# Three of seven block products on 512 columns at once, and one of them a tile later, in a two-layer encoder on one core

## The chip, the core and the metric

The kernel runs on one core of a Trainium2 chip. The metric is device time in microseconds, the median of the timed runs. All its arithmetic is float32; matrix products run in TensorE's fp32r format, and each operand is split into a high part (rounded to fp32r) and a low part (the rest), so that a product is three matmuls: high by high, high by low and low by high.

## The reference, cut to what matters

Two layers of a transformer on 512 tokens of width 1024, each with a gated feed-forward, a mixing block with three kinds of attention, and a second feed-forward. The change lies in the four feed-forwards (two a layer), whose inner width is 2816:

```python
def rms_norm(x, g):
    xf = x.astype(jnp.float32)
    y = xf * lax.rsqrt(jnp.mean(xf * xf, axis=-1, keepdims=True) + EPS)
    return (y * g.astype(jnp.float32)).astype(x.dtype)

def swiglu(h, w_gate, w_up, w_down):
    return (jax.nn.silu(h @ w_gate) * (h @ w_up)) @ w_down
...
        h = rms_norm(x, norm_g[l, 0])
        x = x + 0.5 * swiglu(h, ffn_w_gate[l, 0], ffn_w_up[l, 0], ffn_w_down[l, 0])
```

## The kernel before, in words

Features lie on the 128 partitions and tokens along the free axis: an activation is 8 tiles of 128 x 512. The inner width is cut into 22 tiles of 128 (`MF`), and `ffn` (line 275) goes through them. The first two (in the first feed-forward four) are computed plainly, a gate and an up product of 512 columns each. All others, 18 in the first feed-forward and 20 in each of the three others, 78 in all, go through `seven` (line 418).

`seven` computes a tile's gate and up rows for both halves of the tokens (256 each, `H`) as a two-by-two block product: the gate and up weights, split over the two halves of the 1024 input features, are one matrix of four blocks, the activations another. It does so in seven block products instead of eight, in the manner of Strassen and Winograd. The weights' sums come in by an accumulating DMA (`added`, line 408) and two additions on VectorE (lines 446 and 447); the activations' sums are made once a feed-forward (`Sides`, line 368). Each block product (`block_product`, line 456) has four chunks of 128 features: per chunk a matmul of high weights with the high tokens (line 460) and one with the low tokens (line 461), both 256 columns wide and with the same weights, and then four of the low weights with the high tokens (line 463). That is 12 matmuls of 256 columns a product and 84 a tile.

Three sets of weights are cast a tile (`parted`, line 91): the high part on ScalarE (line 95), the low part on VectorE (line 96). They are called here wa (the gate's weights), w31 (the sums from the DMA) and w24 (the sums made on VectorE, which need wa's buffer). A fourth, half as large, w22, is cast at lines 436 and 437. The results are combined by copies on ScalarE (lines 474, 483, 485), additions on VectorE (487, 490, 491), a multiplication by the tokens' scale (494), Silu on ScalarE (495), the gating (496), and the split of the result into high and low (`keep`, lines 119 and 121), which the down projection reads.

PSUM has eight banks of 2 KB a partition. The tag `mm` has three of them, `s` and `t` two each. A bank holds 512 float32 columns, two block products side by side.

Each engine takes its instructions in the order in which they stand in its queue. That order is set when the program is built, by a scheduler that reorders within what dependencies and the `issue_after` marks allow; a reader of a PSUM bank waits for the last matmul of the product that was put into it. Where an instruction of a queue waits, what stands behind it waits too.

The down projection (lines 336 to 348) reads all 22 tiles, in three chunks of 8, 8 and 6 for each of 8 output tiles; the last feed-forward has its own form of it in `finish` (line 599).

## Time and profile before

| what | value |
|---|---|
| timed runs, median | 2421.22 us (2420.89 to 2421.51, 3 runs) |
| profiled execution, span from its first to its last instruction (the page gives no other time for it) | 2419.2 us |
| TensorE busy | 2404.9 us (99%), 14418 matmuls |
| weight load busy | 2138.0 us (88%) |
| VectorE busy | 1652.9 us (68%) |
| ScalarE busy | 1254.9 us (52%) |
| GpSimd busy | 270.2 us (11%) |
| granted TensorE clock, mean | 0.998 |

In a row of the timeline stand the start in us, the length in us, the engine, the line, the operation, the tiles (out<-in), their shapes and a count. A matmul's recorded length runs beyond the start of the next one, since they are pipelined; what a matmul costs is the distance from its start to the next one's. The same holds for VectorE and ScalarE: the next instruction starts a little before the recorded end of the one ahead, unless it has to wait for it. In brackets stands how long the engine was idle, and what released it.

### The profile page before, as it was taken

The page shows a single profiled execution, that of the slowest core. Times are in us where ns is not written, and L with a number is a line of the kernel's source. Part 1 is how long each engine was busy: PE and PEld are TensorE (multiplying, and loading weights), DVE is VectorE, ACT ScalarE, POOL GpSimd, SP SyncE. Part 2 cuts the span into 40 slices and gives each one's busy share as a digit, 9 for nine tenths or more (in the row PEclk, how much of TensorE's full clock was granted, in tenths as well). Part 3 has the DMA queues.
Part 4 walks back from the last instruction along what each step waited for, and adds up shares of the span by engine and source line. Part 5 has one row for each costly group of instructions (what it writes and reads, how often), then busy time and mean ns, then how long its engine had stood idle before and what let it go on. Part 6 is the DMA issues. An engine that isn't in the chain of part 4 may idle for free.

```text
span 2419.2 us, 37505 instructions
## 1 busy us (share of the span) xinstructions
PE 2404.9 (99%) x14418; PEld 2138.0 (88%) x14418; DVE 1652.9 (68%) x2767; ACT 1254.9 (52%) x2277; POOL 270.2 (11%) x404
## 2 busy tenths in 40 slices
PE   9999999999999999999999999999999999999998
PEld 7999888888888889998899998888888888999987
DVE  7888445766666678884398873467666666888832
ACT  6555225756567445552255552367566674555532
POOL 3100003311000010000010000133110000100000
PEclk9999999999999999999999999999999999999999
DMA  6675444432332457664367754443322324577632
GB/s 198 174 186 162 128 135 124 115 98 80 94 88 80 131 160 183 185 157 143 119 179 183 183 151 131 127 129 104 101 83 87 95 94 131 168 181 182 175 114 70
DMA packets 113298, 327.19 MB, mean 135 GB/s; under 512 B 13464, under 2 KB 18888, under 8 KB 113120
## 3 DMA queue, kind: packets, MB, share of 16 engines
q1 hardware_dynamic: 88896, 247.04, 33.1%
q0 software_dynamic: 23072, 75.90, 14.4%
q8 instruction: 114, 1.87, 0.3%
q10 hardware_dynamic: 1152, 1.86, 0.2%
q14 instruction: 64, 0.52, 0.1%
HBM read 302.69 MB, written 12.62 MB: 130 GB/s over the span
## 4 chain that ended last, share of the span: by engine, by line
PE 98%; ACT 1%; DVE 0%; issue 0%; DMA 0%; SPq 0%; POOLq 0%; POOL 0%; DVEq 0%; ACTq 0%
PE mm L112 9%; PE mm L110 9%; PE mm L109 9%; PE mm L344 5%; PE mm L345 5%; PE mm L347 5%; PE pr L463 5%; PE pr L460 5%; PE mm L460 5%; PE mm L461 5%; PE mm L463 5%; PE pr L461 5%; PE av L847 2%; PE mm L1065 2%; PE mm L1061 2%; PE mm L1060 2%
## 5 line engine op out<-in xcount | busy, mean ns | idle before, releaser
L87 ACT CAST whi<-raw 128x1024 fp32r<-128x1024 f32 (+1 forms) x258 | 265.7, 1031 | 420.9 <-PE mm L345 184.8
L88 DVE TENSOR_TENSOR wlo<-raw,whi 128x1024 fp32r<-128x1024 f32 (+1 forms) x258 | 309.5, 1201 | 229.1 <-ACT whi L87 121.5
L109 PE MATMUL mm<-h,whi 128*128 128x512 f32 x800 | 318.5, 398 | 0.0
L110 PE MATMUL mm<-l,whi 128*128 128x512 f32 x800 | 313.9, 392 | 0.0
L96 DVE TENSOR_TENSOR wlo<-raw,whi 128x1024 fp32r<-128x1024 f32 x156 | 191.1, 1225 | 83.1 <-ACT whi L95 82.9
L345 PE MATMUL mm<-g,whi 128*128 128x512 f32 x528 | 205.4, 389 | 0.0
L344 PE MATMUL mm<-g,whi 128*128 128x512 f32 x528 | 205.4, 389 | 0.0
L112 PE MATMUL mm<-h,wlo 128*128 128x512 f32 x800 | 197.7, 389 | 0.0
L112 PEld LDWEIGHTS mm<-h,wlo 128*128 128x128 f32 x800 | 150.2, 188 | 31.3
L110 PEld LDWEIGHTS mm<-l,whi 128*128 128x128 f32 x800 | 150.5, 188 | 29.1 <-DVE l L141 0.5
L109 PEld LDWEIGHTS mm<-h,whi 128*128 128x128 f32 x800 | 150.4, 188 | 29.0 <-ACT h L139 0.6
L95 ACT CAST whi<-raw 128x1024 fp32r<-128x1024 f32 x156 | 163.9, 1050 | 10.1 <-DMA raw<-in_w_gu 8.0
L460 PE MATMUL pr<-side,whi 128*128 128x256 f32 x624 | 156.5, 283 | 0.0
L461 PE MATMUL pr<-side,whi 128*128 128x256 f32 x624 | 156.5, 283 | 0.0
L461 PE MATMUL mm<-l,whi 128*128 128x256 f32 x624 | 156.5, 283 | 0.0
L460 PE MATMUL mm<-h,whi 128*128 128x256 f32 x624 | 156.4, 283 | 0.0
L415 POOL DMA_DIRECT2D wsum<-in_w_gu x78 | 68.0, 872 | 686.9 <-DVE g L121 255.7
L347 PE MATMUL mm<-g,wlo 128*128 128x512 f32 x528 | 131.4, 389 | 0.0
L474 ACT COPY gu<-mm 128x256 f32<-128x256 f32 x78 | 29.0, 372 | 195.3 <-PE mm L463 195.2
L806 ACT ACTIVATE lg<-lg,negm 128x256 f32<-128x256 f32 (+1 forms) x192 | 114.2, 595 | 26.7 <-DVE negm L803 25.5
L461 PEld LDWEIGHTS mm<-l,whi 128*128 128x128 f32 x624 | 119.8, 192 | 0.2
L460 PEld LDWEIGHTS mm<-h,whi 128*128 128x128 f32 x624 | 119.8, 192 | 0.2
(306 smaller groups left out, 6130.1 us busy)
## 6 DMA issues: line engine op xcount, KB each, us to landing
raw<-in_w_gu SPq DMA_DIRECT2D x94, 512.0 KB, 3.7
wsum<-in_w_gu SPq DMA_DIRECT2D x78, 512.0 KB, 4.1
wsum<-in_w_gu POOLq DMA_DIRECT2D x78, 512.0 KB, 6.6
raw<-in_w_down SPq DMA_DIRECT2D x48, 512.0 KB, 3.6
raw<-in_w_gate SPq DMA_DIRECT2D x48, 512.0 KB, 3.6
raw<-in_w_qk SPq DMA_DIRECT2D x44, 512.0 KB, 3.6
a<-in_w_gu SPq DMA_DIRECT2D x78, 256.0 KB, 4.8
raw<-in_w_branch SPq DMA_DIRECT2D x24, 512.0 KB, 3.5
```

The lines of the kernel that those rows point to most:

```text
L87: nc.scalar.copy(hi[:, w], raw[:, w])
L88: lower[:] = [nc.vector.tensor_tensor(out=lo[:, w], in0=raw[:, w], in1=f(hi[:, w]), op=ALU.subtract).ins]
L96: nc.vector.tensor_tensor(out=lo, in0=src, in1=f(hi), op=ALU.subtract)
L109: nc.tensor.matmul(ps, wh, xhi[k], start=k == 0, stop=False)
L110: nc.tensor.matmul(ps, wh, xlo[k], start=False, stop=False)
L112: nc.tensor.matmul(ps, wl, xhi[k], start=False, stop=k == n - 1)
L344: nc.tensor.matmul(ps, w[k][0], ghi[c + k], start=c + k == 0, stop=False)
L345: nc.tensor.matmul(ps, w[k][0], glo[c + k], start=False, stop=False)
L347: nc.tensor.matmul(ps, w[k][1], ghi[c + k], start=False, stop=c + k == MF - 1)
L460: nc.tensor.matmul(ps, wh[k], bh, start=start and k == 0, stop=False, skip_group_check=True)
L461: nc.tensor.matmul(ps, wh[k], bl, start=False, stop=False, skip_group_check=True)
L463: nc.tensor.matmul(ps, wl[k], bh, start=False, stop=stop and k == 3, skip_group_check=True)
```

## The change

High and low parts of the tokens, which were two tiles, are now two halves of one tile of 128 x 2 x 512 (`both`), and the same holds for the activations' sums (`two`, `both` in `Sides`). A matmul can so read 256 columns of the high part and 256 of the low part in one go, as 512 columns with the same weights: it writes both to one PSUM bank, the high part's result in the left half and the low part's in the right half. The halves are added afterwards, by a copy on ScalarE and an addition on VectorE. Three of the seven products are done like this (`wide`), with 4 matmuls of 512 columns and 4 of 256 instead of 12 of 256. Four products go one after the other through one bank, `one`: the first, the second after that is copied out, a third, and at last the product of w22, which is the wide one and stands in the next tile (`rest`, called by `flush`). With it the gating and the split of a tile's result move into the next tile, and for the last tile into the down projection.

Per tile, 84 matmuls become 72. On VectorE one addition of 256 columns and two of 512 become six of 256; on ScalarE three copies of 256 become five. The sets of weights, their casts and all transfers are as before.

```diff
         def parts(self, k, xk):
             g = self.gain[:, k : k + 1]
-            hi = xpool.tile([P, S], F32R, tag=f"h{k}", name=f"h{k}")
+            both = self.both[k] = xpool.tile([P, 2, S], F32R, tag=f"h{k}", name=f"h{k}")
+            hi, lo = both[:, 0], both[:, 1]
             nc.scalar.activation(hi, xk, AF.Copy, scale=g)
-            lo = xpool.tile([P, S], F32R, tag=f"l{k}", name=f"l{k}")
...
                 for c, n, w in parts:
+                    if m == 0 and c == 8:
+                        tiles.flush()
                     for k in range(n):
...
+            two = fp.tile([P, 2, S], F32R, tag="pair", name="pair", bufs=4)
+            self.halves(one.rearrange("p a c -> p (a c)"), two)
+            both = fp.tile([P, 2, H], F32R, tag="side", name="side", bufs=4)
+            self.halves(t3, both)
+            self.t = [two[:, :, :H], two[:, :, H:], both]
+            self.b11, self.b21, self.b22 = h.both[e][:, :, :H], h.both[o][:, :, :H], h.both[o][:, :, H:]
+            self.t4, self.b12 = t4, h.both[e][:, :, H:]
...
+        def product(self, bank, w, b, start=False, stop=False, wide=True):
...
+            (wh, wl), (ps, both) = w, (bank[:, 0], bank)
...
+            def mm(dst, k, w, b):
+                nc.tensor.matmul(dst, w[k], b, start=start and k == 0 and w is wh and b is not low, stop=False, skip_group_check=True)
...
+            for k, bk in enumerate(b):
+                low = bk[:, 1]
+                if wide:
+                    mm(both, k, wh, bk)
+                else:
+                    mm(ps, k, wh, bk[:, 0])
+                    mm(ps, k, wh, low)
+            for k, bk in enumerate(b):
+                nc.tensor.matmul(ps, wl[k], bk[:, 0], start=False, stop=stop and k == 3, skip_group_check=True)
...
+            self.product(one, blocks(wa), [s.b11 for s in sides], start=True, wide=False)
+            kept = nc.scalar.copy(c11, one[:, 0])
...
+            self.product(two, blocks(w31, S), self.side(1), start=True)
+            nc.scalar.copy(c22, two[:, 1])
+            nc.vector.tensor_tensor(out=c22, in0=two[:, 0], in1=c22, op=ALU.add)
+            done = self.flush()
+            w22 = [fp.tile([P, S], F32R, tag=g, name=g) for g in ("w22h", "w22l")]
+            nc.scalar.copy(w22[0], a22)
+            nc.vector.tensor_tensor(out=w22[1], in0=a22, in1=f(w22[0]), op=ALU.subtract)
+            self.product(one, blocks(w24), self.side(2), wide=False)
+            self.held = [nc.scalar.copy(c12, one[:, 0]).ins]
+            self.product(three, blocks(wa, S), [s.b21 for s in sides], start=True, stop=True, wide=False)
+            nc.vector.tensor_tensor(out=c11, in0=three[:, 0], in1=c11, op=ALU.add)
+            self.product(two, blocks(w24, S), [s.b22 for s in sides], stop=True)
+            for n in range(2):
+                nc.vector.tensor_tensor(out=c12, in0=two[:, n], in1=c12, op=ALU.add)
+            self.product(one, blocks(w31), self.side(3), wide=False)
+            nc.scalar.copy(u3, one[:, 0])
+            gn = g[:, 0:2].rearrange("p a c -> p (a c)")
+            un = g[:, 3:5].rearrange("p a c -> p (a c)")
+            nc.vector.tensor_tensor(out=gn, in0=gn, in1=h.rb, op=ALU.mult)
+            nc.scalar.activation(gn, gn, AF.Silu)
+            nc.vector.tensor_tensor(out=c22, in0=c22, in1=u3, op=ALU.add)
...
+            def rest():
+                self.product(one, blocks(w22), self.side(4), stop=True)
+                nc.scalar.copy(c21, one[:, 1])
+                nc.vector.tensor_tensor(out=c21, in0=one[:, 0], in1=c21, op=ALU.add)
+                last = nc.vector.scalar_tensor_tensor(out=un, in0=un, scalar=-1.0, in1=gn, op0=ALU.mult, op1=ALU.mult)
+                keep(fp, un, *self.out)
+                return last.ins
```

In the changed file the lines are: the matmuls of high weights 437, those of low weights 447; the copies of c11 494, c22 501, c12 508, u3 515 and c21 524; Silu 519; w22's casts 505 and 506; the additions 502, 510, 513 (twice), 520 and 525; the scale 518 and the gating 526; the sums of weights 478 and 479.

The order of ScalarE's queue in a tile in the middle of the second feed-forward, before. A name's number tells the buffers apart: gu_10943 belongs to the tile that is being finished, gu_11069 to the tile that is being computed; whi from raw with the lower number is w24, with the higher number the next tile's wa. In brackets stand the engines and transfers waited for.

```order
L95 CAST whi_11056<-wsum_11041 128x1024 [waits DMAHW0_49,DMASW4_49,Activation_49]
L474 COPY gu_11069<-mm_11066 128x256 [waits DVE_49,PE_49]
L495 ACTIVATE gu_10943<-gu_10943 128x512 [waits DVE_49,Activation_49]
L95 CAST whi_11062<-raw_11044 128x1024 [waits DVE_49]
L119 CAST g_11037<-gu_10943 128x512 [waits DVE_49]
L483 COPY gu_11069<-mm_11066 128x256 [waits PE_49]
L95 CAST whi_11174<-raw_11170 128x1024 [waits DMAHW1_49]
L436 CAST w22h_11178<-a22_11172 128x512 [waits DMAHW2_49,PE_49,Activation_49]
L485 COPY pv_11068<-pr_11067 128x256 [waits PE_49]
```

After, a tile of the same kind (gu_10059 is being finished, gu_10178 computed; whi_10171 is w24, whi_10280 the next tile's wa):

```order
L515 COPY gu_10059<-mm_10056 128x256 [waits PE_49]
L519 ACTIVATE gu_10059<-gu_10059 128x512 [waits DVE_49]
L494 COPY gu_10178<-mm_10175 128x256 [waits PE_49,Activation_49]
L505 CAST w22h_10217<-a22_10159 128x512 [waits DMAHW1_49,PE_49]
L501 COPY gu_10178<-pr_10176 128x256 [waits PE_49]
L524 COPY gu_10059<-mm_10056 128x256 [waits PE_49]
L95 CAST whi_10171<-raw_10157 128x1024 [waits DVE_49]
L119 CAST g_10213<-gu_10059 128x512 [waits DVE_49]
L508 COPY gu_10178<-mm_10175 128x256 [waits PE_49]
L95 CAST whi_10280<-raw_10276 128x1024 [waits DMAHW2_49]
L95 CAST whi_10284<-wsum_10273 128x1024 [waits DMAHW3_49,DMASW0_49,Activation_49]
```

The w24 cast stood behind Silu and now stands behind four instructions that wait for TensorE, the last of them the copy of line 524. 48 tiles have these ahead of it; in 26 it stands as in the next tile, between w22's cast and that copy (whi_10290 is w24 there), and the first tile of each feed-forward has no copy of line 524:

```order
L515 COPY gu_10178<-mm_10175 128x256 [waits PE_49]
L519 ACTIVATE gu_10178<-gu_10178 128x512 [waits DVE_49]
L494 COPY gu_10297<-mm_10294 128x256 [waits PE_49,Activation_49]
L501 COPY gu_10297<-pr_10295 128x256 [waits PE_49]
L505 CAST w22h_10336<-a22_10278 128x512 [waits DMAHW4_49,PE_49]
L95 CAST whi_10290<-raw_10276 128x1024 [waits DVE_49]
L524 COPY gu_10178<-mm_10175 128x256 [waits PE_49]
L508 COPY gu_10297<-mm_10294 128x256 [waits PE_49]
```

In the last of these fences the cast moved one place ahead of the copy. On TensorE, where the product with w24 and side 2 begins, before (the end of w22's product, and the first matmuls that need w24):

```order
L463 MATMUL pv_11068<-h1_8398,w22l_11053 128x256
L463 MATMUL pv_11068<-h2_8441,w22l_11053 128x256
L463 MATMUL pv_11068<-h3_8484,w22l_11053 128x256
L460 MATMUL mm_11066<-side_8677,whi_11062 128x256 [waits Activation_49]
L461 MATMUL mm_11066<-side_8679,whi_11062 128x256
```

And after (the end of the product w22 of the tile before, the one product that follows it, and the first matmul that needs w24):

```order
L447 MATMUL mm_10056<-h3_8335,w22l_10099 128x256
L437 MATMUL pv_10177<-h4_8377,whi_10161 128x256 x2
L437 MATMUL pv_10177<-h5_8419,whi_10161 128x256 x2
L437 MATMUL pv_10177<-h6_8461,whi_10161 128x256 x2
L437 MATMUL pv_10177<-h7_8503,whi_10161 128x256 x2
L447 MATMUL pv_10177<-h4_8377,wlo_10162 128x256
L447 MATMUL pv_10177<-h5_8419,wlo_10162 128x256
L447 MATMUL pv_10177<-h6_8461,wlo_10162 128x256
L447 MATMUL pv_10177<-h7_8503,wlo_10162 128x256
L437 MATMUL mm_10175<-pair_8523,whi_10171 128x256 [waits Activation_49]
```

Between the product whose copy stands ahead of the w24 cast on ScalarE and the product that needs this cast there are now 12 matmuls of 256 columns. In the 26 other tiles one of the twelve stands behind the start of the product with w24.

More of the change, by code (lines that the diff above doesn't have):

```diff
@@ L285, in ffn @@
                 sides = []
-            loads, held = [], ()
+            loads = []
             start, plain = (2, 4) if first else (0, 2)
@@ L293, in ffn @@
                             small_values(fp)
+                    if m == plain:
+                        tiles = Seven(l, i, h, fp, sides, ghi, glo)
                     with tc.issue_after(h.marks[1]):
-                        held, gated_last = seven(l, i, m, h, fp, sides, ghi, glo, loads[1], sums if m == plain else None, held)
+                        gated_last = tiles.tile(m, loads[1], sums if m == plain else None)
                     continue
@@ L383, in __init__ @@
             b11, b12, b21, b22 = t[0][:, :H], t[0][:, H:], t[1][:, :H], t[1][:, H:]
-            one, two = [fp.tile([P, 2, H], F32, tag="g", name="tsum", bufs=GBUFS) for _ in range(2)]
-            t1, t2, t3, t4 = one[:, 0], one[:, 1], two[:, 0], two[:, 1]
+            one, other = [fp.tile([P, 2, H], F32, tag="g", name="tsum", bufs=GBUFS) for _ in range(2)]
+            t1, t2, t3, t4 = one[:, 0], one[:, 1], other[:, 0], other[:, 1]
             nc.vector.tensor_tensor(out=t1, in0=b11, in1=b12, op=ALU.subtract)
@@ L585, in x_room @@
     def x_room(fp):
-        side = [fp.tile([P, S], F32, tag="side", name="xt", bufs=12) for _ in range(8)]
-        return [side[2 * t : 2 * t + 2] for t in range(4)]
+        pairs = [fp.tile([P, 2, S], F32, tag="pair", name="xt", bufs=4) for _ in range(4)]
+        return [[t[:, 0], t[:, 1]] for t in pairs]
     def x_turned(xt, k):
@@ L637, in finish @@
             if c == 0:
+                tiles.flush()
                 xt = x_room(fp)
```

139 lines of the change are left out of this document (56 added, 83 removed).

## The prediction

> **What bounds the kernel now.** I read the page first, for its shares and for the chain that ended last.
>
> ```profile
> span 2419.2 us, 37505 instructions
> PE 98%; ACT 1%; DVE 0%; issue 0%; DMA 0%; SPq 0%; POOLq 0%; POOL 0%; DVEq 0%; ACTq 0%
> L474 ACT COPY gu<-mm 128x256 f32<-128x256 f32 x78 | 29.0, 372 | 195.3 <-PE mm L463 195.2
> ```
>
> TensorE is the whole chain, and line 474, which runs once a tile, counts 78 tiles of the kind that the change rewrites. The spans cover 2419.2 us; the timed runs have a median of 2421.22 us, so 2.0 us lie around the span, and I add my sum to the median. Then the windows, for the pace of one stage: two inside the seven-product tiles, one inside the down projection.
>
> ```profile
> 150.00:190.00 40.00, 40.00 (x336) 40.00 (x335) 34.94 (x48) 22.27 (x36) 3.49 (x4) 1.00 0.74 188
> 250.00:290.00 40.00, 40.00 (x178) 33.11 (x177) 16.62 (x20) 11.62 (x14) 2.72 (x5) 1.00 0.42 128
> 204.00:214.08 10.08, 10.08 (x86) 10.08 (x85) 8.80 (x13) 5.56 (x10) 0.70 (x1) 1.00 0.68 184
> ```
>
> After the length stand TensorE, weight load, VectorE, ScalarE and GpSimd. In the first window TensorE starts 336 matmuls of 256 columns in 40 us, 0.119 each with no gap; a tile is 84 of them, 10.08 us. VectorE is busy for 8.80 of that, ScalarE for 5.56, and the clock is granted in full. So a tile lasts as long as its matmuls take to start. Third, the timeline where the last tile meets the down projection, for the price of each width:
>
> ```profile
> 237.49 0.28 PE L460 MATMUL pr<-h,whi 128*128 128x256 f32 x1
> 237.61 0.28 PE L461 MATMUL pr<-l,whi 128*128 128x256 f32 x1
> 237.73 0.64 PE L463 MATMUL pr<-h,wlo 128*128 128x256 f32 x4
> 238.21 0.40 PE L344 MATMUL mm<-g,whi 128*128 128x512 f32 x1
> ...
> 239.14 0.39 PE L344 MATMUL mm<-g,whi 128*128 128x512 f32 x1
> ...
> 240.05 0.39 PE L344 MATMUL mm<-g,whi 128*128 128x512 f32 x1
> ...
> 307.14 1.98 PE L347 MATMUL mm<-g,wlo 128*128 128x512 f32 x8
> ```
>
> The first number is the start. A narrow matmul takes 0.12 (237.49 to 237.61). The first four wide ones behind narrow ones take 0.93 together (238.21 to 239.14), the first eight 1.84 (to 240.05), and in a long run one takes (1.98 - 0.39) / 7 = 0.227.
>
> **The change, part by part.** In what follows P1 to P7 are the tile's products in their new order: P1 (wa with b11), P2 (wide, side 1), P3 (wide, the tile before's w22 with side 4), P4 (b21, bank three), P5 (w24 with side 2), P6 (wide, b22), P7 (w31 with side 3).
>
> *TensorE's saving.* Three products swap four pairs each for four wide matmuls: 12 pairs a tile, 936 in all. P2's and P3's wide ones stand nearly together in the built order, P6's alone. By the rows for runs of eight and four that is 8 x 0.24 - 1.84 = 0.08 and 4 x 0.24 - 0.93 = 0.03, so 0.11 a tile and 8.6 us in 78. By the long run's 0.227 it would be 12 x 0.013 x 78 = 12.2 us. I take 8.6, because each short run here follows narrow matmuls as the rows at 238.21 do; 12.2 stays an end of the range. No row shows a wide matmul that reads its columns in two pieces of 256, as these do; if that alone took the gain away, this term would be 0.
>
> The Trainium skill's page "TensorE: Matmul & The Clock Gate", section "Back-to-back issue gap", gives N / 2.4 + 2.5 ns per matmul, that is 109 ns at 256 columns and 216 ns at 512; an estimate from it is 2.5 ns a pair, 2.3 us in all, and the kernel would then come out at 2433. The rows here show 120 and 227, so a merged pair saves 13 in the long run.
>
> *The wait that it adds.* w24 is cast on ScalarE (line 95) and P5 starts on it. Before, that cast is early:
>
> ```profile
> 201.44 1.05 ACT L95 CAST whi<-raw 128x1024 fp32r<-128x1024 f32 x1
> ...
> 205.09 0.28 PE L460 MATMUL mm<-side,whi 128*128 128x256 f32 x1
> ```
>
> It ends at 202.49 and is used at 205.09, 2.6 us later. After, in 48 of the 78 tiles of the built order, the cast stands on ScalarE right behind the copy of line 524, which waits for P3's last matmul; P4 alone lies between P3 and P5 on TensorE. The lags are in this stretch:
>
> ```profile
> 203.17 0.64 PE L463 MATMUL mm<-h,wlo 128*128 128x256 f32 x4
> 203.65 0.28 PE L460 MATMUL pv<-h,w22h 128*128 128x256 f32 x1
> ...
> 203.85 0.37 ACT L483 COPY gu<-mm 128x256 f32<-128x256 f32 x1 [0.84 <-PE mm L463]
> ...
> 204.12 1.05 ACT L95 CAST whi<-raw 128x1024 fp32r<-128x1024 f32 x1
> ...
> 205.07 0.62 ACT L436 CAST w22h<-a 128x512 fp32r<-128x512 f32 x1
> ...
> 205.59 0.38 ACT L485 COPY pv<-pr 128x256 f32<-128x256 f32 x1
> ```
>
> The product of line 463 gives up its place at 203.65, its copy starts at 203.85 (0.20 later), the cast behind it 0.27 later, and takes 1.05. What a matmul pays when its operand is late is shown once in the tiles before:
>
> ```profile
> 106.57 0.37 ACT L485 COPY pv<-pr 128x256 f32<-128x256 f32 x1
> ...
> 106.73 0.28 PE L461 MATMUL pr<-side,whi 128*128 128x256 f32 x1
> ...
> 106.99 0.39 PE L460 MATMUL pr<-h,whi 128*128 128x256 f32 x1
> 107.21 0.28 PE L461 MATMUL pr<-l,whi 128*128 128x256 f32 x1
> 107.33 0.29 PE L460 MATMUL pr<-h,whi 128*128 128x256 f32 x1
> ```
>
> The copy ends at 106.94, the matmul that was due at 106.85 starts at 106.99, 0.05 behind it, and the next needs 0.22 instead of 0.12: a stall costs its length and 0.10. So from P3's end to P5's start the chain needs 0.20 + 0.27 + 1.05 + 0.05 = 1.57 against P4's 12 x 0.12 = 1.44. Short by 0.13, plus 0.10, is 0.23 a tile; in 48 tiles 11.0 us.
>
> In the 26 other tiles that carry a P3, the copy stands behind the w24 cast, but w22's cast (line 505) stands ahead of it, and that waits until P3's wide matmuls have read the buffer that it refills. From there: 0.20 + 0.52 (205.07 to 205.59) + 1.05 + 0.05 = 1.82, against P3's four narrow ones and eleven of P4's, 15 x 0.12 = 1.80. Short by 0.02, plus 0.10: 0.12 a tile, 3.1 us. Behind the late cast on ScalarE are the casts of the finished tile and of the next weights and the copy of line 508, for which P7 waits; on VectorE w24's low part and all behind it.
>
> *VectorE.* Its rows give the spacing of each size:
>
> ```profile
> 206.34 0.69 DVE L437 TENSOR_TENSOR w22l<-a,w22h 128x512 fp32r<-128x512 f32 x1
> 206.94 0.42 DVE L487 TENSOR_TENSOR gu<-mm,gu 128x256 f32<-128x256 f32 x1
> 207.28 1.22 DVE L96 TENSOR_TENSOR wlo<-wsum,whi 128x1024 fp32r<-128x1024 f32 x1
> 208.41 0.68 DVE L490 TENSOR_TENSOR gu<-pr,gu 128x512 f32<-128x512 f32 x1
> ...
> 211.65 0.69 DVE L496 SCALAR_TENSOR_TENSOR gu<-gu 128x512 f32<-128x512 f32 x1 [0.15 <-ACT gu L495]
> 212.62 1.23 DVE L96 TENSOR_TENSOR wlo<-raw,whi 128x1024 fp32r<-128x1024 f32 x1 [0.27 <-ACT whi L95]
> ...
> 215.28 1.23 DVE L96 TENSOR_TENSOR wlo<-raw,whi 128x1024 fp32r<-128x1024 f32 x1 [0.84 <-ACT whi L95]
> ```
>
> That is 0.60 for 512 columns, 0.34 for 256, 1.13 for 1024. A tile before has three of 1024, eight of 512 and one of 256: 8.53. After it has three, six and six: 9.03. TensorE's tile after is about 10.08 - 0.11 + 0.19 = 10.16 (0.19 is 14.1 us over 74 tiles), so VectorE's work alone hides, with 1.13 left for its waits; their price is a rival below. ScalarE gains two copies of 0.27 and stays near 6.1 of 10.16; they cost only through the chain above.
>
> *What I cost at nothing.* The bank of P1, P5, P7 and the late P3 is held into the next tile; there are three such banks and two are in use at once. The common tile for high and low parts changes neither the opening's waits nor the DMAs: SP and GpSimd issue the same transfers in the same order, and w22's transfer, now used most of a tile later, has two buffers. The last tile's P3 stands in the down projection behind 24 wide matmuls, and its result is needed 34 wide matmuls later (7.7 us at 0.227), against about 3 us for its copy, two adds, cast and subtraction; without that cover four feed-forwards would pay up to 3 us each.
>
> The sum: -8.6 + 11.0 + 3.1 = +5.5, so 2421.2 + 5.5 = 2426.7 us.
>
> **Rivals.** *The cast is in time (faster).* If the chain to P5 were 0.23 shorter, 1.34 instead of 1.57, stall and restart would both go, and the saving stays: 2421.2 - 8.6 = 2412.6, down to 2409.0 with the long run's price. For it: the margin is a sixth of the chain, and nothing else on TensorE is late before. Against: the order on ScalarE is fixed, and each length in it comes from a row of the same shape.
>
> *VectorE becomes the pace.* If its waits stay at the 0.15 + 0.27 + 0.84 = 1.26 that the rows show, its tile is 9.03 + 1.26 = 10.29, 0.21 over 10.08, and the kernel takes 2421.2 + 78 x 0.21 = 2437.6. It decides from waits of 1.13 a tile. For it: two adds now follow directly on what they read, and its queue waits for P2, P3 and P6 through copies. Against: most of the 1.26 is the 0.84 that it waits because it is early, and that shrinks when it gets late.
>
> *Merging saves nothing (it doesn't do what it says).* If a wide matmul in two pieces costs what its pair did, only the waits stay: 2421.2 + 14.1 = 2435.3. The rule of the Trainium skill's page "TensorE: Matmul & The Clock Gate", section "Back-to-back issue gap", comes close to this. For it: no row has such a read. Against: the rows of whole 512 columns are plain on the price.
>
> **How the numbers follow.** About 0.2%, 4.8 us, is what a measurement of this kernel can tell from no change, so "same" is 2416.4 to 2426.1. My forecast has 0.52; its bounds (8.6 or 12.2 saved, restarts paid in full or in part) run from about 2420 to 2432, so 0.27 of it is slower, 0.23 same and 0.02 faster. The cast in time has 0.25, all faster. VectorE as the pace has 0.13, all slower. Merging that saves nothing has 0.10, 0.08 of it slower and 0.02 same. That is faster 0.27, same 0.25, slower 0.48. The range has to take in the case on the other side: from 2410.0, which leaves out only the largest saving, to 2438.0, which takes in both slow cases.
>
> The likeliest case's own range is 2420 to 2432.
>
> **What would show it.** In the changed kernel's timeline a tile should last about 10.15, with one gap on TensorE ahead of the first matmul of P5 (its start 0.25 instead of 0.12 behind that of the last of P4, and 0.22 to the next), and the list of waits should charge it to ScalarE's cast of line 95, in some 70 tiles. The copy of line 524 should start 0.20 behind P3's end and the cast 0.27 later. The wide matmuls should start 0.23 apart. I am wrong if P5 follows P4 without a gap (then the first rival), if VectorE has no idle time left in a tile and TensorE waits for low parts of weights (the second), or if wide matmuls stand 0.24 apart (the third).

## The result, and the profile after

The changed kernel takes 2435.3 us (median of four runs, 2434.3 to 2436.8) against 2421.3 us before (2420.9 to 2421.5): 1.0058 times as long, with a 95% interval of 1.0044 to 1.0073. It is slower by 14 us. The forecast had 2426.7 us and slower as the likeliest sign; the time lies in its range, 8.6 us above the 2426.7, and 3.3 above the 2420 to 2432 that it gave as the likeliest case's own.

The page of the changed kernel, its span and its chain:

```profile
span 2434.1 us, 36014 instructions
PE 96%; DVE 1%; ACT 1%; DMA 0%; issue 0%; SPq 0%; POOLq 0%; POOL 0%; ACTq 0%; DVEq 0%
```

TensorE's share of the chain has fallen from 98% to 96%. The two windows of the forecast, and a longer one in the tiles of the third feed-forward (the second layer's first), after (columns as in the forecast):

```profile
150.00:190.00 40.00, 40.00 (x286) 37.29 (x285) 36.43 (x59) 23.88 (x42) 3.48 (x4) 1.00 0.72 184
250.00:290.00 40.00, 40.00 (x178) 33.14 (x177) 15.33 (x18) 11.57 (x15) 2.72 (x5) 1.00 0.38 118
1300.00:1400.00 100.00, 100.00 (x706) 92.78 (x706) 92.78 (x148) 61.08 (x108) 7.84 (x9) 1.00 0.70 180
```

The same long window before:

```profile
1300.00:1400.00 100.00, 100.00 (x835) 100.00 (x835) 87.33 (x121) 55.55 (x90) 8.71 (x10) 1.00 0.70 185
```

The down projection is untouched (178 matmuls in 40 us, as before). In the seven-product tiles VectorE goes from 87 to 93 of 100 us. TensorE is shown as wholly busy in both, because a recorded matmul reaches over a short gap. The weight load falls from full to 93%, but that is no measure of the gaps either: in e9 below, whose tiles have none in this window, it is at 95%, since a matmul of 512 columns has one load as one of 256 has. So I add up, over a whole trace, the distance from the start of each matmul of these tiles to the start of the next: 787.7 us before, 803.0 after, 15.3 more. The spans differ by 14.9 and the timed runs by 14.0, so the loss lies in these tiles.

The timeline around P5 in a tile of the third feed-forward, the place that the forecast names:

```profile
1304.83 0.69 DVE L479 TENSOR_TENSOR raw<-raw 128x512 f32<-128x512 f32 x1
...
1305.04 0.64 PE L447 MATMUL mm<-h,w22l 128*128 128x256 f32 x4
...
1305.52 1.12 PE L437 MATMUL pv<-h,whi 128*128 128x256 f32 x8
...
1305.72 0.37 ACT L524 COPY gu<-mm 128x256 f32<-128x256 f32 x1
1305.99 1.05 ACT L95 CAST whi<-raw 128x1024 fp32r<-128x1024 f32 x1
...
1306.48 0.64 PE L447 MATMUL pv<-h,wlo 128*128 128x256 f32 x4
...
1307.10 0.51 PE L437 MATMUL mm<-pair,whi 128*128 128x256 f32 x2
```

P3 gives up its place at 1305.52. The copy starts 0.20 later and the cast 0.27 after that; it ends at 1307.04 and P5 starts 0.06 behind it. P5 was due at 1305.52 + 1.44 = 1306.96, so it is 0.14 late by these rows (0.134 in the trace's nanoseconds), and its second matmul needs 0.10 more than 0.12. The chain is the one that the forecast worked out, link by link. Over the whole trace 45 tiles have this gap (0.13 to 0.14), 27 have a smaller one (0.02 to 0.09), four early tiles of a feed-forward have single gaps of 0.23 to 1.87 us, and two have none of 0.02 or more. Between 1290 and 1400 us a tile takes 10.22 us on the mean, where the forecast had 10.15.

The list of TensorE's waits has only the few long ones, since a matmul's record reaches over a short gap (line waited at, engine and line waited for, us in all, times, longest):

```profile
PE mm L437 <- ACT whi L95: 2.6, 3, 1.7
PE mm L447 <- DVE wlo L96: 1.9, 4, 0.6
```

The second row was not in the forecast: low parts of weights, from VectorE, come late too. Their usual form is short, as here at P2's low part in every third tile of this stretch:

```profile
1323.06 1.09 PE L437 MATMUL pr<-pair,whi 128*128 128x512 f32 x4
...
1323.80 1.22 DVE L96 TENSOR_TENSOR wlo<-wsum,whi 128x1024 fp32r<-128x1024 f32 x1
...
1323.99 1.07 PE L437 MATMUL mm<-h,w22h 128*128 128x512 f32 x4
...
1324.90 0.28 PE L447 MATMUL mm<-h,w22l 128*128 128x256 f32 x1
...
1325.07 0.54 PEld L447 LDWEIGHTS pr<-pair,wlo 128*128 128x128 f32 x4 [0.21 <-DVE wlo L96]
```

w31's low part is ready at 1325.02, when its first matmul is due, and that starts at 1325.07; 0.05 and the 0.10 behind it. I count as a stall what a start is more than 0.015 late, against the median for its pair of widths. In the whole trace the stalls ahead of and within P5's high part come to 18.7 us (11.0 of gaps and 7.7 of restarts), those at low parts to 8.2, and the rest to 0.6.

### The profile page after: what moved, and what is told of

Its sections match the earlier page's. It is cut to its first block, busy times and chain, and to the rows that moved or that the text cites. A ratio compares the mean times of both kernels' runs of the same rounds, so it can differ in the third digit from the quotient of the medians.

```text
span 2434.1 us, 36014 instructions
## 1 busy us (share of the span) xinstructions
PE 2416.8 (99%) x13482; PEld 2092.2 (86%) x13482; DVE 1702.6 (70%) x3001; ACT 1307.5 (54%) x2433; POOL 269.2 (11%) x404
## 4 chain that ended last, share of the span: by engine, by line
PE 96%; DVE 1%; ACT 1%; DMA 0%; issue 0%; SPq 0%; POOLq 0%; POOL 0%; ACTq 0%; DVEq 0%
PE mm L437 13%; PE mm L112 9%; PE mm L110 8%; PE mm L109 8%; PE mm L447 6%; PE pr L437 6%; PE mm L349 5%; PE mm L348 5%; PE mm L351 5%; PE pr L447 3%; PE pv L437 3%; PE av L881 2%; PE mm L1099 2%; PE mm L1095 2%; PE mm L1094 2%; PE pv L447 1%
## 5 line engine op out<-in xcount | busy, mean ns | idle before, releaser
L109 PE MATMUL mm<-h,whi 128*128 128x512 f32 x800 | 318.5, 398 | 0.0
L110 PE MATMUL mm<-h,whi 128*128 128x512 f32 x800 | 313.9, 392 | 0.0
L96 DVE TENSOR_TENSOR wlo<-raw,whi 128x1024 fp32r<-128x1024 f32 x156 | 190.5, 1221 | 14.1 <-ACT whi L95 13.5
L110 PEld LDWEIGHTS mm<-h,whi 128*128 128x128 f32 x800 | 150.5, 188 | 29.1 <-DVE h L141 0.5
L109 PEld LDWEIGHTS mm<-h,whi 128*128 128x128 f32 x800 | 150.4, 188 | 29.1 <-ACT h L140 0.6
L351 PEld LDWEIGHTS mm<-g,wlo 128*128 128x128 f32 x528 | 99.1, 188 | 20.6
L349 PEld LDWEIGHTS mm<-g,whi 128*128 128x128 f32 x528 | 99.1, 188 | 20.5
L348 PEld LDWEIGHTS mm<-g,whi 128*128 128x128 f32 x528 | 99.1, 188 | 20.4
L119 ACT CAST g<-gu 128x512 fp32r<-128x512 f32 x88 | 54.7, 621 | 98.8 <-DVE gu L526 89.1
L437 PE MATMUL mm<-pair,whi 128*128 128x256 f32 x624 | 95.0, 295 | 2.7 <-ACT whi L95 2.6
L437 PE MATMUL pr<-h,whi 128*128 128x512 f32 x312 | 97.1, 394 | 0.0
L96 DVE TENSOR_TENSOR wlo<-wsum,whi 128x1024 fp32r<-128x1024 f32 x78 | 95.0, 1218 | 0.0
```

The source lines that it names most:

```text
L96: nc.vector.tensor_tensor(out=lo, in0=src, in1=f(hi), op=ALU.subtract)
L109: nc.tensor.matmul(ps, wh, xhi[k], start=k == 0, stop=False)
L110: nc.tensor.matmul(ps, wh, xlo[k], start=False, stop=False)
L348: nc.tensor.matmul(ps, w[k][0], ghi[c + k], start=c + k == 0, stop=False)
L349: nc.tensor.matmul(ps, w[k][0], glo[c + k], start=False, stop=False)
L351: nc.tensor.matmul(ps, w[k][1], ghi[c + k], start=False, stop=c + k == MF - 1)
```

## The experiments

Each comparison is with the kernel before on the same chip, so ratios are what to compare; the changed kernel has 1.0058. Theories A and B are those of the first four kernels (e1, e2, e4, e5; A: the copies ahead of w24's cast are the whole cause; B: VectorE's queue is as near to its end), C and D those formed after them (C: the wait is a loop from P5's copy through the next wa's cast and VectorE's sums to the next P5; D: the amount of VectorE's work).

**Merging alone (e10).** The tile is written in the old order and with the old banks, and its products of w31 with side 1, w22 with side 4 and w24 with b22 are issued wide:

```diff
+            self.product(pr, blocks(w31, S), self.side(1), start=True)
+            self.product(pr[:, 1:2], blocks(w31), self.side(3), wide=False)
+            self.product(pa, blocks(wa, S), [s.b21 for s in sides], wide=False)
+            mine = nc.scalar.copy(c11, pa[:, 0])
+            self.product(pv, blocks(w22), self.side(4), start=True, stop=True)
...
+            self.product(pr, blocks(w24, S), [s.b22 for s in sides], stop=True)
...
+            self.held = [mine.ins]
```

> One part of the change alone: the common tiles for high and low parts, and the same three products issued with 512 columns, but in the order of the kernel before, each sum in its old bank, nothing carried into the next tile, VectorE's and ScalarE's steps as before. The low parts' sums of the wide products fall into a neighbouring half bank and aren't added to the right result; that part of the computation is left out, all other work is as before. Theory C (merging saves 7.8 us and the rest is the new order's waits): ratio to the kernel before 0.9960 to 0.9975. If merged reads of two pieces saved nothing: 0.999 to 1.001. If the earlier VectorE load (8.5 us a tile) already limited the tiles, something between.

Measured: 2408.1 us against 2418.8, ratio 0.9956 [0.9943, 0.9968]. Two wide products with a narrow one between, on TensorE:

```profile
1303.40 1.09 PE L437 MATMUL pr<-h,whi 128*128 128x512 f32 x4
1304.33 0.63 PE L447 MATMUL pr<-h,wlo 128*128 128x256 f32 x4
1304.80 1.12 PE L437 MATMUL mm<-h,whi 128*128 128x256 f32 x8
1305.75 0.64 PE L447 MATMUL mm<-h,wlo 128*128 128x256 f32 x4
1306.23 1.09 PE L437 MATMUL pr<-pair,whi 128*128 128x512 f32 x4
```

The wide product lasts from 1303.40 to 1304.80, 1.40 us, the narrow one 1.43, and a tile (from 1300.57, where the wide w22 product starts, to 1310.51 in the same list) 9.94. The starts add up to 776.4 us, 11.2 less than before, and of stalls 1.0 us is left, 0.7 of it the same single gap and restart as in the kernel before. So merging is worth 11 us of TensorE's time, and what the new order costs is 803.0 - 776.4 = 26.6 us of waiting. This kernel leaves out the adding of the low halves, so what those additions would cost in the old order isn't shown.

**Merging undone (e2).** The changed kernel's order and banks, and two narrow matmuls where it has a wide one:

```diff
-                    mm(both, k, wh, bk)
+                    mm(ps, k, wh, bk[:, 0])
+                    mm(bank[:, 1], k, wh, low)
```

> The changed kernel with the merging alone undone: each wide matmul is two of 256 columns, the high part into the left half of the bank and the low part into the right half; copies, additions, chain and the late product stay. By the trace of the changed kernel a wide matmul takes 0.2316 us on the mean against 2 x 0.12: 936 x 0.0084 = 7.9 us slower if nothing else moves, 2443 us; with some of the waits for VectorE gone in a longer tile, 2440 to 2443. The rival that merging saves nothing: 2433 to 2436 us.

Measured: 2447.3 us, ratio 1.0119 [1.0105, 1.0133], 0.6% above the changed kernel, and more than the 2440 to 2443 us expected. Merging saves in the new order too; the rival by which it saves nothing falls, from both sides. Its starts add up to 816.1 us, 13.1 above the changed kernel, but its stalls at low parts have grown from 8.2 to 12.9 us, so the 13.1 are not the merging alone.

**The cast ahead of the copies (e1).** The mark `issue_after` puts w22's cast and the copy of line 524 behind w24's cast:

```diff
-        nc.scalar.copy(hi, src)
+        cast[:] = [nc.scalar.copy(hi, src).ins]
...
-            nc.scalar.copy(w22[0], a22)
+            with tc.issue_after(cast[0]):
+                nc.scalar.copy(w22[0], a22)
...
-                nc.scalar.copy(c21, one[:, 1])
+                with tc.issue_after(cast[0]):
+                    nc.scalar.copy(c21, one[:, 1])
```

> The changed kernel (2435.3 us) with w24's cast ahead of the late copy (line 524) and of w22's cast on ScalarE, in every tile; VectorE's work is unchanged. Theory A (the late cast behind the copies is the whole cause, 18.4 us of gaps ahead of P5 in the changed kernel's trace): nearly all of these go, 2415 to 2419 us. Theory B (VectorE's queue is as near to the end of its time: in the built order the sums for w24 stand behind both additions of P6, a low part, the split of the finished tile, the scale, an addition and another low part; from P6's end to P5's start that is 0.20 + 0.34 + 0.46 + 1.14 + 0.60 + 0.60 + 0.34 + 1.14 + 0.72 + 0.68 + 0.10 + 1.05 + 0.15, and P5 and P6 take 2.83, 10.3 a tile): the cast now waits for its sums, P5 is late all the same, 2432 to 2441 us.

Measured: 2443.3 us, ratio 1.0101 [1.0086, 1.0117]. It got slower, and theory A, by which the gap goes with the copies ahead of the cast, falls as it stood. Theory B has the direction and the tile (10.3 us expected); the time lies above its range too. The timeline of e1 at P5 (its lines: cast 97, low parts 98, sums 480 and 481, copies 503 and 528 for 501 and 524):

```profile
1298.74 0.69 DVE L481 TENSOR_TENSOR raw<-raw 128x512 f32<-128x512 f32 x1
...
1299.47 1.05 ACT L97 CAST whi<-raw 128x1024 fp32r<-128x1024 f32 x1
...
1300.51 0.42 DVE L513 TENSOR_TENSOR gu<-pv,gu 128x256 f32<-128x256 f32 x1 [0.73 <-PE pv L449]
1300.57 0.53 PEld L439 LDWEIGHTS mm<-pair,whi 128*128 128x128 f32 x4 [0.30 <-ACT whi L97]
...
1300.85 1.22 DVE L98 TENSOR_TENSOR wlo<-raw,whi 128x1024 fp32r<-128x1024 f32 x1
```

The copy is out of the way, and the cast now starts 0.04 behind the sum that it reads (1298.74 + 0.69 = 1299.43). Meanwhile VectorE stands still for 0.73: next in its queue is an addition that waits for P4, behind it the low part that waits for the cast. From that addition to the next tile's last sum it works 9.3 us with hardly a pause, then comes the cast, then P5, and P4 of the next tile follows P5 at TensorE's own pace. This is a loop around VectorE, ScalarE and TensorE that takes two tiles once round: 10.08 from P5 to the end of the next tile's P4, 0.20 to the addition, 9.28 on VectorE, and 0.04 + 1.05 + 0.05 through the cast to P5. That is 20.70, and a tile lasts 10.36 us in this stretch. In the changed kernel the sum of the tile shown above ended at 1305.52, 0.47 ahead of the cast, and in the tile ahead of it 0.13: two limits, the second close behind the first.

**One addition on GpSimd (e4 and e5).** e4 is e1 with line 520 on GpSimd. e5 is the changed kernel with that and with w24's cast marked behind the copy of line 524 in every tile that has one; the cast is written further down for this, so w24's low part moves in VectorE's queue too.

```diff
-            nc.vector.tensor_tensor(out=c22, in0=c22, in1=u3, op=ALU.add)
+            nc.gpsimd.tensor_tensor(out=c22, in0=c22, in1=u3, op=ALU.add)
...
+            if not first:
+                with tc.issue_after(self.copied):
+                    w24 = parted(raw)
```

> The cast first as in e1, and one addition a tile (c22 += u3, 256 columns, both operands in SBUF) on GpSimd instead of VectorE, which takes 0.34 us a tile off VectorE's queue and lets the scheduler put the sums for w24 earlier. Theory A and theory B both expect the gaps ahead of P5 and the waits for low parts to go: before's 2421.3 less what merging saves, 7.9 to 9.3 us, so 2412 to 2415 us. If something else in the change costs (the chained bank, the product a tile later), it stays above 2418.

> The opposite pair: the addition on GpSimd as in e4, so VectorE has the same relief, but w24's cast is held behind the late copy in all 74 tiles that have one. Theory A: each tile still pays 0.13 to 0.17 and 0.10 ahead of P5, 17 to 20 us, against 8 to 9 saved: 2429 to 2433 us. If VectorE's load alone is the cause, it is as fast as e4: 2412 to 2415 us.

Measured: e4 2432.2 us, ratio 1.0056 [1.0043, 1.0068]; e5 2485.8 us, ratio 1.0275 [1.0261, 1.0289]. Both miss all that was expected of them. e4 is below e1 by 0.45%, which says that VectorE's work counts there, but not ahead of the changed kernel. e5's loss was in neither theory. Its low parts of w31, the shortest, the median and the longest in ns:

```profile
L96 DVE TENSOR_TENSOR wlo<-raw,whi x156: 1211/1221/1227, 46.4 to 2345.6; 128x1024 fp32r<-128x1024 f32 x156
...
L96 DVE TENSOR_TENSOR wlo<-wsum,whi x78: 1203/1766/1773, 48.7 to 2339.9; 128x1024 fp32r<-128x1024 f32 x78
```

The same subtraction takes 1.22 us for w24 and wa and 1.77 for w31, beside which GpSimd's addition runs (1.09 us of it, 78 times). The 0.34 us taken off VectorE cost it 0.55. That is 0.21 a tile, while a tile of e5 is 0.74 longer than one of the changed kernel (10.94 against 10.20); the rest isn't isolated. The Trainium skill's page "GPSIMD Engine Reference", section "1. Specifications", says that GpSimd shares VectorE's interface to SBUF, with contention where VectorE reads two inputs from SBUF; this subtraction reads two, and the trace of e5 agrees. In e4 the same two instructions meet in another order:

```profile
1311.63 1.22 DVE L98 TENSOR_TENSOR wlo<-wsum,whi 128x1024 fp32r<-128x1024 f32 x1
1312.14 1.30 POOL L523 TENSOR_TENSOR gu<-gu 128x256 f32<-128x256 f32 x1 [3.20 <-issue]
...
1313.09 0.90 DVE L480 TENSOR_TENSOR raw<-wsum,raw 128x512 f32<-128x512 f32 x1
```

There the subtraction starts first and keeps its 1.22, as in nearly all tiles of e4; the addition takes 1.30, and the sum that starts beside it 0.90 instead of 0.68. In both kernels the one that starts second gets longer. So these two runs don't decide between the theories.

**Two additions less on VectorE (e12).** e1, without the second addition of line 513 and without line 520:

```diff
-            for n in range(2):
-                nc.vector.tensor_tensor(out=c12, in0=two[:, n], in1=c12, op=ALU.add)
+            nc.vector.tensor_tensor(out=c12, in0=two[:, 0], in1=c12, op=ALU.add)
...
-            nc.vector.tensor_tensor(out=c22, in0=c22, in1=u3, op=ALU.add)
```

> e1 (w24's cast ahead of both copies, all else as in the changed kernel, the next wa's cast still behind P5's copy), and VectorE does two additions of 256 columns less in each tile: the low half of bank two to c12 and the addition of u3 to c22 are left out of the computation, 0.68 us of VectorE's queue a tile; ScalarE and TensorE do the same work as in e1, in nearly the same order. Theory C, now with VectorE's queue as the long part of the loop (P5, its copy, the next wa's cast, VectorE's queue to the sums, w24's cast, P5: 10.2 to 10.3 us in e1): the loop gets 0.68 shorter, the gaps of 0.26 + 0.10 a tile ahead of P5 go, and the ratio to the kernel before is 0.996 to 0.999, against 1.010 in e1. If ScalarE's order and its waits make the loop, whatever VectorE does: 1.006 to 1.010.

Measured: 2427.6 us, ratio 1.0030 [1.0020, 1.0041]. Both expectations miss: VectorE's queue is the long part of the loop, as 0.7% less than e1 shows, but the loop gave back only 0.2 of the 0.68 us a tile (10.36 to 10.15 us), because VectorE now waits 1.4 us a tile, for P2's copy, for the cast and for P4 (0.52, 0.52 and 0.37). Work taken off an engine in a loop turns partly into waits there.

**The next weights earlier (e6, and e7 with e1's edit).** The chain that leads to VectorE's sums begins with the next wa, whose cast is held back behind the copy of line 508, that is behind P5. It is now held behind w22's cast (in e7 behind line 494's copy):

```diff
-            nc.scalar.copy(w22[0], a22)
+            self.held = [nc.scalar.copy(w22[0], a22).ins]
...
-            self.held = [nc.scalar.copy(c12, one[:, 0]).ins]
+            nc.scalar.copy(c12, one[:, 0])
```

> The changed kernel, but the cast of the next tile's weights wa waits for w22's cast of this tile instead of for the copy of P5's result (line 508); in the built order w24's cast then stands ahead of line 524's copy in most tiles, still behind w22's cast. Theory C (a loop: P5, its copy, the next wa's cast, its low part, the sums, w24's cast, the next P5, with no slack left): the waits of low parts and the 0.13 gaps go, the 0.07 gap behind w22's cast stays in all tiles, so 0.17 a tile for 74 tiles: about 12 us less than the changed kernel, ratio to the kernel before 0.999 to 1.002. Theory D (VectorE's 9.0 to 9.3 us of work in a tile of 10.2 is by itself the pace): no gain, ratio 1.004 to 1.006.

> As the run before, and w24's cast is also put ahead of both copies that stood in front of it on ScalarE (as in e1); the next wa's cast waits for line 494's copy. Theory C: what held e1 back was the loop, so the gaps ahead of P5 go and only single stalls of some 3 to 5 us in all stay; 8 us saved less those: ratio to the kernel before 0.9965 to 0.999. Theory D: VectorE stays the pace, ratio 1.004 to 1.010 as in e1.

Measured: e6 2425.2 us, ratio 1.0020 [1.0011, 1.0029]; e7 2431.2 us, ratio 1.0048 [1.0035, 1.0061]. e6 gains 0.4% on the changed kernel by one mark, and lies at the upper end of what theory C gave. In its timeline at P5 the cast stands ahead of the copy and behind w22's cast:

```profile
1305.41 0.39 PE L437 MATMUL mm<-h,w22h 128*128 128x512 f32 x1
...
1305.83 0.62 ACT L505 CAST w22h<-a 128x512 fp32r<-128x512 f32 x1 [0.56 <-PE mm L437]
...
1306.36 1.05 ACT L95 CAST whi<-raw 128x1024 fp32r<-128x1024 f32 x1
...
1307.31 0.36 ACT L524 COPY gu<-mm 128x256 f32<-128x256 f32 x1
...
1307.45 0.54 PEld L437 LDWEIGHTS mm<-pair,whi 128*128 128x128 f32 x4
```

P3's wide matmuls end their place at 1305.63, 0.20 later w22's cast starts, 0.53 after that w24's, and P5 at 1307.45, 1.82 behind 1305.63: this is the forecast's second chain, to 0.01, and the gap is 0.025 in the tiles of this stretch, with no low part late. Over the whole trace the stalls at low parts fall from 8.2 to 1.3 us, those at P5's high part from 18.7 to 11.1. e7 misses theory C's range and lies in theory D's. Its trace has the sums again at the end of VectorE's queue, behind line 520 and w31's low part, the cast 0.04 behind them and VectorE still for 0.77, a loop like that of e1 with a tile of 10.23 us; here the low part that waits for the cast stands first in VectorE's queue.

**The sums earlier (e8), and both (e9).** Lines 518 to 520 are written into the late part, so that the scheduler can put the next tile's sums ahead of them:

```diff
-            nc.vector.tensor_tensor(out=gn, in0=gn, in1=h.rb, op=ALU.mult)
-            nc.scalar.activation(gn, gn, AF.Silu)
-            nc.vector.tensor_tensor(out=c22, in0=c22, in1=u3, op=ALU.add)
...
             def rest():
+                nc.vector.tensor_tensor(out=gn, in0=gn, in1=h.rb, op=ALU.mult)
+                nc.scalar.activation(gn, gn, AF.Silu)
+                nc.vector.tensor_tensor(out=c22, in0=c22, in1=u3, op=ALU.add)
```

> The changed kernel, with the next wa's cast as it is there, but the scaling of line 518, the Silu and the addition of line 520 are written behind the next tile's sums (at the head of the late part), so that VectorE does the sums of lines 478 and 479 and w24's cast gets them without waiting for P7's copy; w24's cast stands ahead of lines 524 and 505 in the built order. Theory C: P5's copy to w24's cast is then about 6.7 us of 8.5, so the gaps go: ratio 0.9965 to 1.000. Theory D: the same VectorE work, ratio 1.004 to 1.006.

> The edits of e6 and e8 together. Theory C: no gap ahead of P5 nor ahead of low parts in the steady tiles, 10.0 us a tile; ratio 0.9960 to 0.9985, the kernel faster than both. Theory D: ratio 1.004 to 1.006.

Measured: e8 2435.7 us, ratio 1.0066 [1.0053, 1.0078]; e9 2419.7 us, ratio 1.0000 [0.9991, 1.0009]. e8 misses; its time is that of the changed kernel, near theory D's. Its loop can be read off the timeline, from P5's copy to the next w24 cast:

```profile
1300.17 0.37 ACT L508 COPY gu<-mm 128x256 f32<-128x256 f32 x1 [1.30 <-PE mm L447]
...
1300.44 1.06 ACT L95 CAST whi<-raw 128x1024 fp32r<-128x1024 f32 x1
...
1301.54 1.23 DVE L96 TENSOR_TENSOR wlo<-raw,whi 128x1024 fp32r<-128x1024 f32 x1 [0.33 <-ACT whi L95]
...
1306.28 0.69 DVE L479 TENSOR_TENSOR raw<-raw 128x512 f32<-128x512 f32 x1
...
1306.71 0.64 ACT L521 ACTIVATE gu<-gu 128x512 f32<-128x512 f32 x1
...
1307.24 1.04 ACT L95 CAST whi<-raw 128x1024 fp32r<-128x1024 f32 x1
```

The copy waits for P5, the next wa's cast for the copy, its low part for the cast, and from there to the last sum VectorE works without a pause (1301.54 to 1306.97); Silu then stands ahead of the cast. The edit did half of what it was for: one sum went ahead of the scale of line 518, the other still stands behind it. From the copy it is 7.1 us to the cast's start, where the expectation had about 6.7, and from P5's end, 0.20 ahead of the copy, 8.3 to the cast's end. P5 itself, 1.84 here with the end of P4 in it, and 0.05 to its start close the loop at 10.20 us a tile. e9 cuts it at both places. Around its P5:

```profile
1305.22 0.69 DVE L479 TENSOR_TENSOR raw<-raw 128x512 f32<-128x512 f32 x1
...
1306.33 1.05 ACT L95 CAST whi<-raw 128x1024 fp32r<-128x1024 f32 x1
...
1307.42 1.22 DVE L96 TENSOR_TENSOR wlo<-raw,whi 128x1024 fp32r<-128x1024 f32 x1 [0.57 <-ACT whi L95]
...
1308.19 0.64 PE L447 MATMUL mm<-h,w22l 128*128 128x256 f32 x4
...
1308.67 0.52 PE L437 MATMUL mm<-pair,whi 128*128 128x256 f32 x3
```

The cast ends at 1307.38, 1.3 ahead of P5; a tile lasts 9.96 us with no gap. The long window of e9:

```profile
1300.00:1400.00 100.00, 100.00 (x726) 94.72 (x725) 93.26 (x152) 63.09 (x112) 8.42 (x10) 1.00 0.76 185
```

VectorE is as busy as in the changed kernel, 93 of 100 us, and TensorE starts 726 matmuls where that starts 706. So VectorE's amount of work is not the pace at 9.96 us a tile; theory D falls, and theory C holds for the steady tiles of three feed-forwards. Yet e9 is no faster than the kernel before, and outside both theories' ranges. Its starts add up to 788.3 us, 11.9 above e10, with 5.5 us in five single gaps. The rest is mostly in the first feed-forward, where eleven tiles still take 10.20 us. ScalarE there, up to P5:

```profile
190.96 0.37 ACT L501 COPY gu<-pr 128x256 f32<-128x256 f32 x1 [1.03 <-PE pr L447]
191.23 0.64 ACT L521 ACTIVATE gu<-gu 128x512 f32<-128x512 f32 x1
...
191.76 1.04 ACT L95 CAST whi<-raw 128x1024 fp32r<-128x1024 f32 x1
```

In these tiles the copy that waits for P2 and the Silu stand ahead of w24's cast, which ends at 192.80; P5 starts at 192.85, 0.08 late. With the restart and 0.08 at P5's low part that is 0.26 a tile, 2.9 us in eleven.

**The early tiles (e11).** The largest of the single gaps, 2.55 us, stands in the first feed-forward. Behind it the granted clock is 0.50 (the last three columns are clock, DMA share and GB/s), and the starts are 0.21 and 0.43 us apart instead of 0.12 and 0.23; that costs 1.5 us more:

```profile
100.11:103.40 3.29, 3.29 (x13) 3.10 (x14) 3.29 (x5) 2.63 (x4) 0.00 (x0) 0.50 0.84 134
```

ScalarE ahead of this gap, in e9 (line 521 is the Silu):

```profile
95.69 1.28 ACT L521 ACT_TABLE_LOAD   x1
96.98 0.63 ACT L521 ACTIVATE gu<-gu 128x512 f32<-128x512 f32 x1
97.63 1.28 ACT L258 ACT_TABLE_LOAD   x1
...
99.03 1.03 ACT L95 CAST whi<-raw 128x1024 fp32r<-128x1024 f32 x1
```

The exponentials of some small tables (line 258) and the Silu need different function tables, 1.28 us a load, and w24's cast comes behind them, though its sum is there at 95.97. In the changed kernel the same place has the gap of 1.87, there because VectorE does the small tables' steps ahead of the sum, which ends at 100.52 when P5 was due at 99.8. In the first tile of a feed-forward w24's cast comes behind four casts for side 4. e11 is e9 with both put right:

```diff
+                    w24 = others()
                     for s in sides:
                         s.last()
-                    w24 = others()
...
-                nc.scalar.activation(gn, gn, AF.Silu)
+                with tc.issue_after(cast[0]):
+                    nc.scalar.activation(gn, gn, AF.Silu)
```

> The kernel of e9, and two edits for its single stalls: in the first tile of a feed-forward w24's sums and cast go ahead of the four small casts for side 4, and the Silu (with its table loads in the tile after the small tables) waits until w24's cast is issued. The trace of e9 shows five stalls of 0.4 to 2.6 us there, 5.5 in all. Theory C: 3 to 5 us less than e9, ratio to the kernel before 0.9980 to 0.9990, faster than both. If the time is instead lost to something that no gap ahead of P5 shows: 1.000 as e9.

Measured: 2413.2 us against 2418.8, ratio 0.9974 [0.9964, 0.9984], faster than both kernels and a little better than expected. The starts add up to 781.7 us, 6.0 less than before, where the timed runs have 5.6 less.

## Why the prediction came out as it did

*Merging.* The step was right in kind and too low: 11.2 us instead of 8.6, within the 12.2 that it gave as an end. The wide matmuls cost what the rows of the down projection said (0.93 for four), so reading the columns in two pieces costs nothing that shows. What was not in those rows is that the narrow ones behind them come a little closer, 0.47 for four instead of 0.48, and in e10 a whole narrow product takes 1.433 instead of 1.440. By the Trainium skill's page "TensorE: Matmul & The Clock Gate", section "Back-to-back issue gap", an estimate was 2.3 us; that section gives the formula for an isolated matmul, and e10's 11.2 decide against its use for this stream.

*The wait ahead of P5.* The first chain is exact: 0.134 for 0.13, its restart 0.10, in 45 tiles for 48. The second, for the other tiles, was mostly 0.06 to 0.07 instead of 0.02 in the changed kernel and 0.025 in e6, where nothing else disturbs it; what adds the 0.04 to 0.05 in the changed kernel I haven't isolated. With the single gaps in early tiles, which the forecast didn't have, the term is 18.7 us instead of 14.1. The single gaps are the larger part of the difference.

*VectorE.* This is the step that failed: "so VectorE's work alone hides, with 1.13 left for its waits". The work does hide, as e9 shows, but in the changed order its results don't come in time: low parts of weights cost about 8 us that the sum doesn't have (half of the sign that the forecast named for its rival on VectorE), and e1 shows that the sums for w24 are the next limit, a tenth of a microsecond behind the first. The rival on VectorE had the size nearly right, 2437.6 us, with the wrong mechanism: it let VectorE's time, work plus waits, be the pace, while e1 and e8 show loops through several queues, in e8 through P5's copy, the next wa's cast and VectorE's queue. In the changed kernel this chain has 0.13 to 0.47 us to spare at the sums, but not at the low parts, as e6 shows. I compared sums of durations, and didn't follow one tile's chain into the next. The change had moved the product whose copy lets the next wa go from the fourth place, with b21, to the one that itself waits for w24.

*The cast in time.* This rival's condition is met in most tiles of e9 and e11, not in the change. By the forecast's own rule a chain 0.13 shorter would have been enough, since the restart goes with the stall; it asked for 0.23. Its floor, 2409.0, is close to what merging alone gives, 0.9956 of 2421.3 or 2410.6; e11 comes to 0.9974 of it, 2415.0, with some 5 us of stalls left. Around the late P3 of the last tiles, which I costed at nothing, the trace shows no stall.

*The range.* The time lies in it, but part of that is luck. The bounds of the likeliest case don't follow from the terms it names: with 8.6 or 12.2 saved and restarts paid in full or not at all they are 2415.8 and 2426.7, so its 2420 to 2432 had no working for the upper end, and the time lies above even that. The third rival's figure, 2435.3, is the measured time by chance: its mechanism, merging that saves nothing, is the one that e2 and e10 rule out.

The sum as it came out: -11.2 for the merging, +18.7 + 8.2 + 0.6 for the stalls, and -1.0 for those that e10 has as well, is 15.3 of matmul starts, against 14.0 in the timed runs and 14.9 in the spans. That leaves 0.4 to 1.3 that I can't place; the timed runs of the changed kernel alone lie 2.6 us apart.

What stays open: the scheduler sets ScalarE's and VectorE's order, and each mark moved more than the step that it named, so no run changed one wait alone but e12, which left out work instead. How the 26.6 us divide between the copies and the loop is known only by where the stalls stand.

## What to carry to other kernels

When a change makes an operand needed earlier, follow the chain that makes it backward through every in-order queue until it reaches the product it feeds, one tile earlier; the loop's length, not any engine's busy share, is the tile's lower bound. A limit removed may have another a tenth of a microsecond behind it, so look at how early the next input was before you put a price on the first. When a merge saves matmul time, time it in the old order first: here that showed 11 us of saving and 27 us of waiting inside one number.

## What the runs showed of the hardware

- A late operand costs TensorE its delay and, in nearly all stalls at full granted clock, 0.10 us more at the second matmul (behind 74 of the 76 gaps ahead of P5 in the changed kernel); the matmul starts 0.05 us behind the end of the cast that it waited for.
- After the longest gaps ahead of P5 (2.13 us in e7, 2.36 in e1, 2.55 in e9) the granted clock shows 0.50 for 3.41 us, from 0.1 ahead of to 0.6 behind P5's start. After those of 1.06 to 1.87 us in the changed kernel, e2, e5, e6, e8, e9 and e11 it stays at 1.00. What decides it isn't shown.
- Four wide matmuls behind narrow ones start 0.233, 0.236, 0.228 and 0.232 us apart (medians of 233 such groups in e10), in a long run 0.227; the four narrow ones behind them take 0.47 together.
- An addition on GpSimd that started ahead of a VectorE subtraction slowed it from 1.22 to 1.77 us (e5); where the subtraction started first it kept its 1.22, and the addition took 1.30 instead of 1.09 (e4).
